# One written order for the loads of SyncE in the SSD and output stages of a decoder-trunk kernel

## The chip, the cores and the metric

The kernel runs on one core of a Trainium2 chip. The metric is device time in microseconds (us), the median of several runs; a profile of one more execution gives the trace. PE is TensorE, ACT is ScalarE, DVE is VectorE, POOL is GpSimd, and SP is SyncE, which here does nothing but issue DMA loads and stores.

## The reference

One layer of a decoder for two request groups: 256 prompt tokens and 8 x 4 sample tokens, so N = 288 columns, model width 2048 = 16 tiles of 128.

```python
mod = silu(c) @ w_ada + b_ada                    # six parts of 2048: sh1, sc1, g1, sh2, sc2, g2
h = rmsnorm(x, norm1) * (1 + sc1) + sh1
u_pool, z, xbc, dt = split(h @ w_in)             # 512, 1536, 2560, 24
pool_out = pool_mixer(u_pool, ...)               # windows 2, 4, 8, 16, a map per group
ssd_out = ssd_mixer(z, xbc, dt, ...)             # conv, softplus(dt), chunked scan, silu(z), rmsnorm
x = x + g1 * (concat([pool_out, ssd_out]) @ w_out)
h2 = rmsnorm(x, norm2) * (1 + sc2) + sh2
x = x + g2 * (silu(dwconv(h2 @ w_gate)) * (h2 @ w_val) @ w_down)
y = rmsnorm(x, norm_f)                           # and new states of pool, conv, SSD and FFN
```

All of it is float32. The weights are some 300 MB, and each is read once.

## The kernel before

**Products.** A float32 product is made of three passes on PE: ACT casts a raw weight half to `whi` (line 329), DVE subtracts it from the raw half to get `wlo` (line 331), and `mm3` (lines 344 to 346) adds `whi*hi`, `whi*lo` and `wlo*hi`. One "half" is 128 x 1024 numbers, 512 KB, loaded by SP at line 310; it serves 8 k-tiles, 24 matmuls.

**Stages.** (1) The first norm and the six blocks of `xbc` over growing k groups, up to some 174 us of the trace. (2) The last block `xbc6`, begun with `mm_dt` (lines 1136 to 1147: the dt weights, 24 columns, are cast by ACT and subtracted by DVE into one tile `whi_dt`, and 32 matmuls read it). Beside `xbc6` and then beside the projections `uz` (z of the groups 2 and 3, `u` of the pooling groups 1 and 0) run the units of `back`: the convolution, the SSD groups 0 to 3 (`ssd_group`, lines 850 to 982), pooling. (3) The output projection, 16 column tiles `mm_out_0` to `mm_out_15`, whose last four k-tiles are those of the pooling groups. (4) The MLP, to the end.

**The ada chunks.** The last four parts of the modulation weights are read in small pieces beside all this. `ada_visits` (line 464) is a generator: it loads four chunks of 512 KB (two k-tiles, two halves each) into the ring `rawa`, later puts a "visit" on PE (`whole`, line 451: 16 matmuls of 512 columns that read these four chunks in the reverse of the order in which they were loaded), and then loads the next four. In the SSD stage the ring `rawa` has just four slots, so the loads of a visit wait until the visit before it has read its chunks. `adap2` and `adap3` are the two parts of this stage, eight visits each; the chunks of `adap3` are `raw_adap_3_0_0` (k-tile 0, half 0) to `raw_adap_3_15_1`. `adap4` has four visits of eight chunks in the output stage.

**What sets the order.** The program is written as generators that are advanced with credits (`pull`, line 1118); a scheduler then reorders each engine's instructions by its own estimate of when they can run, except where `keep_in_program_order` or `in_order` pins them. SP is one queue: a load that waits for its slot holds up every load behind it. Other rings: `raw` (weight halves; four slots and one more in `sx`), `whi` and `wlo` (two slots each). The SSD states `h0` of a group come in three loads (`load_h0`, line 835).

Of the kernel before, what the change touches and what calls it, by code (L numbers as in the profile page):

```python
# [18 lines left out]
P = 128  # L19
# [34 lines left out]
VA = (5.01 / 28, 11.01 / 62, 0.42)  # L54
AK, AO = 2, 4
KQ = 4

RB1, RB2, RB3 = 1.0, 1.0, 1.0
TK = 5
# [65 lines left out]
def _wide(part):  # L125
    return (KT - KQ) * P // 4 if part == 4 else D // 4

# [46 lines left out]
def kernel(ctx: ExitStack, tc, ins, outs):  # L174
# [129 lines left out]

    wp = [None]

    def load(key, ring="raw", eng=nc.sync):
        off, cols = S.items[key]
        t = wp[0].tile([P, RAWC], F32, tag=ring, name="raw_" + "_".join(map(str, key)))
        eng.dma_start(t[:, :cols], wflat[off:off + P * cols].rearrange("(p n) -> p n", p=P))  # L310
        return t

    queue = deque(_need_order())
    ahead = {}
# [41 lines left out]
    def project_units(key, nk, opnd=None, order=None):  # L356

        name = "_".join(map(str, key))
        ps = pm.tile([P, 512], F32, tag="mm", name="mm_" + name)
        for h, (k0, n) in enumerate(_halves(nk)):  # L360
            hi, lo = ready.pop(key + (h,), None) or split(load(key + (h,)), 0, n * P, f"{name}_{h}")
            for i in range(n):
                k = k0 + i
                ko = order[k] if order else k
                bh, bl = (xhi[0][ko], xlo[0][ko]) if opnd is None else opnd(k)
                mm3(ps[:, :N], hi, lo, i, bh, bl, k == 0, k == nk - 1)
                if k % YK == YK - 1 or k == nk - 1:
                    yield ps
# [92 lines left out]
                    tc.keep_in_program_order(i)  # L461
                n += 1

    def ada_visits(parts, step, ps=None, begun=0, apart=False, own=None):

        plan = [(part, k0) for part in parts for k0 in range(begun, KT, step)]
        ahead, end, done = [], None, [0]

        def chunks(v):
            part, k0 = plan[v]  # L470
            for k in range(k0, k0 + step):
                for h in range(2):
                    eng = nc.sync if own is None or done[0] < own else nc.gpsimd
                    ahead.append((k, h, load(("adap", part, k, h), "rawa", eng)))
                    done[0] += 1
                    if apart:
                        yield
            for _ in range(1 if apart else 3):
                yield

        yield from chunks(0)
        for v, (part, k0) in enumerate(plan):
            if end:
                ada_end(*end)
                end = None
            if k0 == 0:
                ps = pa.tile([P, 512], F32, tag="ada", name=f"adap{part}")
            whole(ps, ahead, step, True, begun, _wide(part))
            ahead.clear()
            if k0 + step == KT:  # L490
                end = part, ada_sb(ps, _wide(part), f"p{part}")
            yield
            if v + 1 < len(plan):
                yield from chunks(v + 1)
        ada_end(*end)
        yield

# [152 lines left out]
        nc.vector.tensor_scalar(csr, vec[:, K_TRI:K_TRI + N], 0.0, None, ALU.mult)  # L650

    def late_states():
        nc.sync.dma_start(poolw, ins["pool_w"])
        n = XT * NB * 3
        st = sx[0].tile([P, n + 4 * NB * 15], F32, name="st")
        nc.sync.dma_start(st, ins["st"])
        stc.append(st[:, 0:n].rearrange("p (g m b l) -> p g m b l", g=4, m=5, b=NB))
        nc.gpsimd.tensor_copy(ups.rearrange("p m b l -> p (m b) l")[:, :, 0:15],
                              st[:, n:].rearrange("p (m l) -> p m l", l=15))
# [92 lines left out]
    def xbc_units(bi):  # L752
        (_, gk), _ = BLOCKS[bi]
        end = bi + 1 == len(BLOCKS)
        for ci, (ks, ms) in enumerate(_xbc_chunks(bi)):
            key = ("xbc", bi, ci)
            hi, lo = ready.pop(key, None) or split(load(key) if end else fetch(key), 0, len(ms) * gk * P,
                                                   f"xbc{bi}_{ci}", bi < GB or end)
            begun = []
            if bi + ci == 0:  # L760
                begun = [aux(f"xbc0_{m}") if m % 2 else pm.tile([P, 512], F32, tag="mm", name=f"xbc0_{m}")
# [70 lines left out]
    ssq = kp.tile([P, N], F32, tag="ssx", name="ssq")  # L832
    sbx = kp.tile([P, P + G6], F32, name="sbx")

    def load_h0(g):
        for i, (b0, nb) in enumerate(HB):
            t = mx.tile([P, 3, G6], F32, tag="blk", name=f"h0_{g}_{i}", bufs=4)
            nc.sync.dma_start(t[:, 0:nb, :], ins["h0"][b0:b0 + nb, :, g, :].rearrange("b p n -> p b n"))
            h0t[g, i] = t

    def h0b(g, b):
# [8 lines left out]
    def ssd_group(g):  # L850
# [120 lines left out]
        if g < ZEARLY:  # L971
            nc.scalar.activation(zy[g], zy[g], AF.Silu)
        dec = [decays(0)]
        yield
        dec.append(decays(1))
        outputs(0, *dec[0])
        yield
        dec.append(decays(2))
        outputs(1, *dec[1])
        yield  # L980
        outputs(2, *dec[2])
        yield
# [124 lines left out]
    def take(gn, n):  # L1107
        for _ in range(n):
            next(gn)
            yield  # L1110

    ssd3 = ssd_group(3)
    back = chain(conv0, h0s(0), zip2(ssd_group(0), conv_group(1)), h0s(1),
                 zip2(ssd_group(1), conv_group(2)), h0s(2), zip2(ssd_group(2), conv_group(3)), h0s(3),
                 zip2(take(ssd3, TK), chain(pool_units(UEARLY[0]), pool_units(UEARLY[1]))))
    credit = {}

    def pull(gn, rate):
# [7 lines left out]
    for bi in range(len(BLOCKS)):  # L1126
        last = bi + 1 == len(BLOCKS)
        top_up()
        if last:

            wp[0].drop(w0)
            wp[0].move("rawa", "raw", "rawa")
            w0_ctx.close()
            sx[0] = mx_ctx.enter_context(tc.tile_pool(name="sx", bufs=1, reuse_waits="tile"))
            wp[0].add(sx[0], "raw", "raw", 1)
            raw = load(("dt",))[:, :KT * NH].rearrange("p (k h) -> p k h", h=NH)
            wdt = wp[0].tile([P, RAWC], F32R, tag="whi", name="whi_dt")
            with tc.high_priority():
                nc.gpsimd.memset(wdt.bitcast(F32), 0.0)
                both = wdt[:, :DTW * KT].rearrange("p (k c) -> p k c", c=DTW)  # L1140
                nc.scalar.copy(both[:, :, 0:NH], raw)
                nc.vector.tensor_tensor(both[:, :, 32:32 + NH], raw, both[:, :, 0:NH].bitcast(F32), ALU.subtract)
            ps = pm.tile([P, 512], F32, tag="mm", name="mm_dt")
            for k in range(KT):
                w = wdt[:, DTW * k:DTW * k + P]
                nc.tensor.matmul(ps[:, :N], w, turns(xhi[0][k]), start=k == 0, stop=False)
                nc.tensor.matmul(ps[:, :N], w, turns(xlo[0][k]), start=False, stop=k == KT - 1)
            late_states()
            next(adas)
# [22 lines left out]
    for m in list(range(4 + 3 * ZEARLY, 16)) + ULATE:  # L1172
# [9 lines left out]
        if m < 4:  # L1182
            late[m] = pool_units(m)
            next(late[m])
    drain(adas)
    wp[0].move("rawa", "rawa", "raw")
    adas = ada_visits((4,), AO, apart=True, own=RAWA + RAW2 + RAW3[1])
    for h, (_, n) in enumerate(_halves(KT)):
        ready[("out", 0, h)] = split(load(("out", 0, h)), 0, n * P, f"out_0_{h}")
    drain(back)  # L1190
    npl = kp.tile([P, 4, 135], F32, tag="hmod", name="npl", bufs=2)
    nc.gpsimd.tensor_copy(npl[:, :, 0:15], upp[:, :, NP:15 + NP])
# [14 lines left out]
    def out_units(m):  # L1207
# [1 line left out]
        pz = pm.tile([P, 512], F32, tag="mm", name=f"mm_out_{m}")  # L1209
        pp = aux(f"mm_outp_{m}")  # L1210
        for h, (k0, n) in enumerate(_halves(KT)):
            hi, lo = ready.pop(("out", m, h), None) or split(load(("out", m, h)), 0, n * P, f"out_{m}_{h}")
# [8 lines left out]
    for i in range(KT // YK):  # L1221
# [10 lines left out]
    wp[0].drop(sx[0])  # L1232
# [53 lines left out]
    for m in range(16):  # L1286
        if m in XM:
            sl = slice(4 * XM.index(m), 4 * XM.index(m) + 4)
            nc.sync.dma_start(x[:, sl, :], ins["x"][:, sl, :])
        if m == 1:  # L1290
            wp[0].move("rawa", "raw", "rawa")
            for ring, tag, n in (("rawa", "raw", RAW2), ("whi", "whi", SPLIT2), ("wlo", "wlo", SPLIT2)):
                wp[0].add(w2, ring, tag, n)
            wp[0].add(w3, "raw", "raw", RAW3[0])
            wp[0].add(w3, "rawa", "rawa", RAW3[1])
        if m == 0:
            out_norm(ps0[0], m)
        else:
# [9 lines left out]
            drain(adas)  # L1308


    for k in range(2):
        ready[("upk", k)] = split(load(("upk", k)), 0, 2 * FK * P, f"upk{k}")
    fill = [load(("adaq", q), "rawa") for q in range(KT // 2)]
# [325 lines left out]
```

## Time and profile before

| | us |
|---|---|
| median of 3 runs (range) | 1263.47 (1262.98 to 1264.55) |
| the profiled execution, its own time | 1261.59 |
| its span, first to last instruction | 1259.8 |
| PE busy | 1243.5 (99%) |
| DVE, ACT, POOL busy | 820.7, 581.7, 243.9 |
| mean granted clock of TensorE | 0.998 |

PE is busy nearly all the time, so the time of this kernel is PE's work plus the moments in which PE waits. The rows further down show where these are.

### The profile page before, as it was taken

What the parts mean: (1) busy time and instruction counts of PE and PEld (TensorE: products, weight loads), DVE (VectorE), ACT (ScalarE), POOL (GpSimd) and SP (SyncE); (2) the same over time, 40 slices, a digit from 0 to 9 for tenths busy, and PEclk for the clock granted to TensorE, in tenths of its full rate; (3) what the DMA queues carried; (4) which work ended last, traced back from release to release, by engine and by line L of the source; (5) the groups of instructions that cost most, each with busy time, mean ns of one, the idle gap of its engine ahead of it and who ended that gap; (6) DMA issues with size and microseconds to landing.
All of it is one profiled execution on the core that took longest, in us unless ns stands there. A gap on an engine that the chain in (4) does not pass through costs nothing.

```text
span 1259.8 us, 26442 instructions
## 1 busy us (share of the span) xinstructions
PE 1243.5 (99%) x10647; PEld 1166.6 (93%) x10647; DVE 820.7 (65%) x1379; ACT 581.7 (46%) x914; POOL 243.9 (19%) x468
## 2 busy tenths in 40 slices
PE   9999999999999999999999999999999999999997
PEld 7899988777789899999999999999999999999996
DVE  5785669888776658654675556666665567576553
ACT  5343345688744335433443334444443344444553
POOL 0000003222225413110221001312220012232221
PEclk9999999999999999999999999999999999999999
DMA  9999788888899974788866556665665665666622
GB/s 377 413 415 373 306 290 329 314 306 321 307 372 406 365 263 154 243 321 322 310 210 197 181 194 201 211 208 196 191 195 184 204 206 199 200 216 209 199 75 76
DMA packets 97419, 323.21 MB, mean 257 GB/s; under 512 B 10896, under 2 KB 20048, under 8 KB 97296
## 3 DMA queue, kind: packets, MB, share of 16 engines
q1 hardware_dynamic: 91872, 303.25, 68.8%
q0 software_dynamic: 4704, 17.17, 3.7%
q8 instruction: 83, 1.36, 0.4%
q10 hardware_dynamic: 720, 1.11, 0.2%
q14 instruction: 40, 0.33, 0.1%
HBM read 309.78 MB, written 10.39 MB: 254 GB/s over the span
## 4 chain that ended last, share of the span: by engine, by line
PE 90%; DMA 5%; DVE 2%; ACT 1%; issue 0%; SPq 0%; POOL 0%; DVEq 0%; ACTq 0%; POOLq 0%
PE mm_down L344 7%; PE mm_down L346 7%; PE mm_down L345 7%; PE mm_gate L344 6%; PE mm_val L344 6%; PE mm_gate L345 6%; PE mm_val L345 6%; PE mm_gate L346 6%; PE mm_val L346 6%; PE xbc L344 4%; PE adap L457 4%; PE xbc L345 4%; PE xbc L346 4%; PE adag L419 2%; DMA raw_adap<-wflat 2%; PE mm_out L344 2%
## 5 line engine op out<-in xcount | busy, mean ns | idle before, releaser
L344 PE MATMUL mm_down<-ah,whi_down 128*128 128x288 f32 x688 | 196.8, 286 | 0.0
L345 PE MATMUL mm_down<-al,whi_down 128*128 128x288 f32 x688 | 196.8, 286 | 0.0
L346 PE MATMUL mm_down<-ah,wlo_down 128*128 128x288 f32 x688 | 196.8, 286 | 0.0
L344 PE MATMUL mm_gate<-h2h,whi_gate 128*128 128x288 f32 x640 | 183.5, 287 | 0.0
L344 PE MATMUL mm_val<-h2h,whi_val 128*128 128x288 f32 x640 | 183.1, 286 | 0.0
L346 PE MATMUL mm_gate<-h2h,wlo_gate 128*128 128x288 f32 x640 | 183.0, 286 | 0.0
L345 PE MATMUL mm_val<-h2l,whi_val 128*128 128x288 f32 x640 | 183.0, 286 | 0.0
L346 PE MATMUL mm_val<-h2h,wlo_val 128*128 128x288 f32 x640 | 183.0, 286 | 0.0
L345 PE MATMUL mm_gate<-h2l,whi_gate 128*128 128x288 f32 x640 | 183.0, 286 | 0.0
L331 DVE TENSOR_TENSOR wlo_down<-raw_down,whi_down 128x1024 fp32r<-128x1024 f32 x96 | 108.4, 1129 | 103.2 <-ACT whi_down L329 103.2
L331 DVE TENSOR_TENSOR wlo_gate<-raw_gate,whi_gate 128x1024 fp32r<-128x1024 f32 x80 | 99.8, 1248 | 107.4 <-ACT whi_gate L329 107.4
L329 ACT CAST whi_down<-raw_down 128x1024 fp32r<-128x1024 f32 x96 | 91.9, 957 | 144.0 <-PE mm_down L345 119.9
L329 ACT CAST whi_gate<-raw_gate 128x1024 fp32r<-128x1024 f32 x80 | 83.5, 1045 | 130.3 <-PE mm_gate L345 65.3
L329 ACT CAST whi_val<-raw_val 128x1024 fp32r<-128x1024 f32 x80 | 83.8, 1047 | 115.2 <-issue 91.3
L344 PEld LDWEIGHTS mm_down<-ah,whi_down 128*128 128x128 f32 x688 | 130.0, 189 | 0.0
L345 PEld LDWEIGHTS mm_down<-al,whi_down 128*128 128x128 f32 x688 | 130.0, 189 | 0.0
L346 PEld LDWEIGHTS mm_down<-ah,wlo_down 128*128 128x128 f32 x688 | 130.0, 189 | 0.0
L344 PE MATMUL xbc<-h1h,whi_xbc 128*128 128x288 f32 x444 | 128.9, 292 | 0.8 <-ACT h1h L258 0.5
L345 PE MATMUL xbc<-h1l,whi_xbc 128*128 128x288 f32 x444 | 127.1, 287 | 0.0
L346 PE MATMUL xbc<-h1h,wlo_xbc 128*128 128x288 f32 x444 | 125.2, 287 | 0.3 <-DVE wlo_xbc L331 0.3
L344 PEld LDWEIGHTS mm_gate<-h2h,whi_gate 128*128 128x128 f32 x640 | 120.9, 189 | 3.4 <-issue 3.4
L345 PEld LDWEIGHTS mm_val<-h2l,whi_val 128*128 128x128 f32 x640 | 121.0, 189 | 0.0
(357 smaller groups left out, 3002.9 us busy)
## 6 DMA issues: line engine op xcount, KB each, us to landing
raw_adap<-wflat SPq DMA_DIRECT2D x96, 512.0 KB, 6.1
raw_gate<-wflat SPq DMA_DIRECT2D x80, 512.0 KB, 4.0
raw_val<-wflat SPq DMA_DIRECT2D x80, 512.0 KB, 3.6
raw_ada<-wflat SPq DMA_DIRECT2D x64, 512.0 KB, 9.4
raw_xbc<-wflat SPq DMA_DIRECT2D x50, 512.0 KB, 9.8
raw_down<-wflat SPq DMA_DIRECT2D x48, 512.0 KB, 3.6
raw_out<-wflat SPq DMA_DIRECT2D x32, 512.0 KB, 10.2
raw_down<-wflat SPq DMA_DIRECT2D x32, 384.0 KB, 3.7
```

The costliest lines, as they stand in the source:

```text
L329: yield nc.scalar.copy(hi[:, :n], raw[:, a:a + n])
L331: yield hi, lo, nc.vector.tensor_tensor(lo[:, :n], raw[:, a:a + n], hi[:, :n].bitcast(F32), ALU.subtract)
L344: nc.tensor.matmul(ps, whi[:, w], bh, start=first, stop=False)
L345: nc.tensor.matmul(ps, whi[:, w], bl, start=False, stop=False)
L346: nc.tensor.matmul(ps, wlo[:, w], bh, start=False, stop=last)
L419: i = nc.tensor.matmul(ps[32 * j:32 * j + 32, :nb], sc_c[:, ck, :], raw[:, c:c + nb], start=q0 + n == 0, stop=q0 + AQ[gi] >= nq and n + 1 ...
L457: i = nc.tensor.matmul(ps[32 * j:32 * j + 32, :w], sc_c[:, k, :], raw[:, w * (j % 2):w * (j % 2) + w], start=not begun and k == step - 1, ...
```

## The change

From block `xbc6` to the end of the output projection the loads of SP are pinned in the order in which the program writes them (`tied`). Two helpers keep that order: `plan` is a list of weight halves still to load, `more(n)` loads until n of them are in `coming`, and `came(key)` takes one. A half of `xbc6` or `uz` that is split is followed by `more(4)`, one of `out` by `more(6)`. The chunks of the next visit are loaded right behind the visit that frees their slots, as before, but their loads now keep their place. `load_h0` is called in thirds from within the SSD group before (the first group's states still come from `h0s(0)`). The extra `raw` slot in `sx` is given up a little earlier, and the rings are enlarged in another order in the output stage.

```diff
+LA, OA = 4, 6
     def load(key, ring="raw", eng=nc.sync):
         off, cols = S.items[key]
         t = wp[0].tile([P, RAWC], F32, tag=ring, name="raw_" + "_".join(map(str, key)))
-        eng.dma_start(t[:, :cols], wflat[off:off + P * cols].rearrange("(p n) -> p n", p=P))
+        i = eng.dma_start(t[:, :cols], wflat[off:off + P * cols].rearrange("(p n) -> p n", p=P))
+        if tied[0] and eng is nc.sync:
+            tc.keep_in_program_order(i)
         return t
+    plan, coming = deque(), {}
+    def more(n):
+        while plan and len(coming) < n:
+            key = plan.popleft()
+            coming[key] = load(key)
+    def came(key):
+        while key not in coming:
+            more(len(coming) + 1)
+        return coming.pop(key)
...
-            hi, lo = ready.pop(key + (h,), None) or split(load(key + (h,)), 0, n * P, f"{name}_{h}")
+            half = key + (h,)
+            got = came(half) if half in coming or half in plan else load(half)
+            hi, lo = split(got, 0, n * P, f"{name}_{h}")
+            more(LA)
...
-    def load_h0(g):
-        for i, (b0, nb) in enumerate(HB):
+    def load_h0(g, which=(0, 1, 2)):
+        for i in which if g < 4 else ():
...
         dec = [decays(0)]
+        load_h0(g + 1, (0,))
         yield
         dec.append(decays(1))
         outputs(0, *dec[0])
+        load_h0(g + 1, (1,))
...
             wp[0].add(sx[0], "raw", "raw", 1)
+            tied[0] = True
             raw = load(("dt",))[:, :KT * NH].rearrange("p (k h) -> p k h", h=NH)
...
+            plan.extend(("xbc", bi, ci) for ci in range(len(_xbc_chunks(bi))))
+            plan.extend(("uz", m, h) for m in list(range(4 + 3 * ZEARLY, 16)) + ULATE for h in range(2))
+            plan.extend(("out", 0, h) for h in range(2))
+            more(LA)
             late_states()
...
     drain(adas)
+    wp[0].drop(sx[0])
     wp[0].move("rawa", "rawa", "raw")
...
-        ready[("out", 0, h)] = split(load(("out", 0, h)), 0, n * P, f"out_0_{h}")
+        ready[("out", 0, h)] = split(came(("out", 0, h)), 0, n * P, f"out_0_{h}")
+    plan.extend(("out", m, h) for m in range(1, KT) for h in range(2))
+    more(LA)
```

What it moves on the engines, at three places. First SP at the end of the ada chunks; `raw_out_m_h` is half h of the output weights of column tile m. Before:

```order
L310 DMA raw_out_0_0_4555<-wflat 128x1024
L310 DMA raw_out_0_1_4561<-wflat 128x1024
L310 DMA raw_adap_3_12_0_4380<-wflat 128x1024
L310 DMA raw_adap_3_12_1_4382<-wflat 128x1024
L310 DMA raw_adap_3_13_0_4384<-wflat 128x1024
L310 DMA raw_adap_3_13_1_4386<-wflat 128x1024
L310 DMA raw_out_1_0_4734<-wflat 128x1024
L310 DMA raw_out_1_1_4766<-wflat 128x1024
L310 DMA raw_adap_3_14_0_4470<-wflat 128x1024
```

Now, the same queue and place:

```order
L313 DMA raw_out_0_0_4296<-wflat 128x1024
L313 DMA raw_adap_3_12_0_4388<-wflat 128x1024
L313 DMA raw_adap_3_12_1_4390<-wflat 128x1024
L313 DMA raw_adap_3_13_0_4392<-wflat 128x1024
L313 DMA raw_adap_3_13_1_4394<-wflat 128x1024
L313 DMA raw_out_0_1_4421<-wflat 128x1024
L313 DMA raw_adap_3_14_0_4476<-wflat 128x1024
L313 DMA raw_adap_3_14_1_4478<-wflat 128x1024
L313 DMA raw_adap_3_15_0_4480<-wflat 128x1024
L313 DMA raw_adap_3_15_1_4482<-wflat 128x1024
L313 DMA raw_out_1_0_4567<-wflat 128x1024
```

Half 1 of `mm_out_0` now stands behind the chunks of the last visit but one, and half 0 of `mm_out_1` behind those of the last; before, each stood ahead of them.

Second PE at the same place; a row with `x2` is two matmuls. Before, the last visit but one (chunks 3_13 and 3_12) stands within `mm_uz_0`, the last `uz` tile, and 55 rows of other matmuls follow until the last visit:

```order
L344 MATMUL mm_uz_0_4457<-h1h11_130,whi_uz_0_0_4460 128x288
L457 MATMUL adap3_3684<-raw_adap_3_13_1_4386,sc_c_85 32x512 x2
L457 MATMUL adap3_3684<-raw_adap_3_13_0_4384,sc_c_85 32x512 x2
L457 MATMUL adap3_3684<-raw_adap_3_12_1_4382,sc_c_85 32x512 x2
L457 MATMUL adap3_3684<-raw_adap_3_12_0_4380,sc_c_85 32x512 x2
L345 MATMUL mm_uz_0_4457<-h1l11_146,whi_uz_0_0_4460 128x288
```

Now it stands behind the first half of `mm_out_0`, and these are the rows from it to the last visit and `mm_out_1`, with `...` for nine more matmuls of `mm_out_0` like those around them:

```order
L364 MATMUL mm_out_0_4635<-mixh11_4590,wlo_out_0_0_4561 128x288
L1051 MATMUL pool1_4532<-pout_4120,poolw_153 128x288
L478 MATMUL adap3_3698<-raw_adap_3_13_1_4394,sc_c_85 32x512 x2
...
L478 MATMUL adap3_3698<-raw_adap_3_12_0_4388,sc_c_85 32x512 x2
L362 MATMUL mm_out_0_4635<-mixh12_4591,whi_out_0_1_4563 128x288
...
L364 MATMUL mm_out_0_4635<-mixh15_4594,wlo_out_0_1_4565 128x288
L478 MATMUL adap3_3698<-raw_adap_3_15_1_4482,sc_c_85 32x512 x2
...
L478 MATMUL adap3_3698<-raw_adap_3_14_0_4476,sc_c_85 32x512 x2
L362 MATMUL mm_out_1_4744<-mixh4_4583,whi_out_1_0_4746 128x288
```

Twelve matmuls of `mm_out_0` are all that PE has between the last two visits.

Third DVE ahead of `mm_dt`. `xbc5_24` to `xbc5_27` are the last four tiles of block `xbc5`, which DVE adds to the rows `zy`; `whi_dt` is the subtraction that completes the dt weights. Before:

```order
L331 TENSOR_TENSOR wlo_xbc5_13_2304<-raw_xbc_5_13_2006,whi_xbc5_13_2302 128x1024
L1142 TENSOR_TENSOR whi_dt_2340<-raw_dt_2338,whi_dt_2340 128x16x24
L784 TENSOR_TENSOR zy0_155<-zy0_155,xbc5_24_2274 128x288
L784 TENSOR_TENSOR zy1_156<-zy1_156,xbc5_25_2288 128x288
L331 TENSOR_TENSOR wlo_xbc6_0_2459<-raw_xbc_6_0_2455,whi_xbc6_0_2457 128x1024
L784 TENSOR_TENSOR zy1_156<-zy1_156,xbc5_26_2306 128x288
L784 TENSOR_TENSOR zy1_156<-zy1_156,xbc5_27_2320 128x288
```

Now:

```order
L349 TENSOR_TENSOR wlo_xbc5_13_2304<-raw_xbc_5_13_2006,whi_xbc5_13_2302 128x1024
L812 TENSOR_TENSOR zy0_155<-zy0_155,xbc5_24_2274 128x288
L812 TENSOR_TENSOR zy1_156<-zy1_156,xbc5_25_2288 128x288
L812 TENSOR_TENSOR zy1_156<-zy1_156,xbc5_26_2306 128x288
L812 TENSOR_TENSOR zy1_156<-zy1_156,xbc5_27_2320 128x288
L1175 TENSOR_TENSOR whi_dt_2340<-raw_dt_2338,whi_dt_2340 128x16x24
L349 TENSOR_TENSOR wlo_xbc6_0_2465<-raw_xbc_6_0_2377,whi_xbc6_0_2463 128x1024
```

`whi_dt` moved behind the addition of the last tile of `xbc5`; on PE the 32 matmuls of `mm_dt` still follow at once on that tile.

## Rows read from the trace of the kernel before

**Rows 1.** The page: the span, and each engine's busy time.

```profile
span 1259.8 us, 26442 instructions
PE 1243.5 (99%) x10647; PEld 1166.6 (93%) x10647; DVE 820.7 (65%) x1379; ACT 581.7 (46%) x914; POOL 243.9 (19%) x468
```

**Rows 2.** Stretches: length, busy us (instructions) by engine, clock, DMA share, GB/s.

```profile
200.00:300.00 100.00, 98.62 (x828) 76.54 (x830) 86.18 (x171) 69.49 (x140) 26.07 (x43) 1.00 0.87 318
300.00:340.00 40.00, 38.69 (x348) 29.14 (x341) 30.26 (x58) 30.98 (x71) 7.37 (x10) 1.00 0.84 312
340.00:360.00 20.00, 19.23 (x156) 15.23 (x152) 18.47 (x42) 14.57 (x27) 5.22 (x10) 1.00 0.87 301
620.00:1240.00 620.00, 620.00 (x5051) 620.00 (x5050) 382.00 (x554) 270.71 (x377) 123.44 (x241) 1.00 0.60 193
```

**Rows 3.** Timeline of DVE at `mm_dt`: start, duration, instruction, idle time before.

```profile
171.30 0.55 DVE L1142 TENSOR_TENSOR whi_dt<-raw_dt,whi_dt 128x384 fp32r<-128x384 f32 x1
...
174.89 0.46 DVE L784 TENSOR_TENSOR zy<-zy,xbc 128x288 f32<-128x288 f32 x1 [0.40 <-PE xbc L346]
```

**Rows 4.** Timeline of PE: the last matmul of `xbc5` and the first of `mm_dt`.

```profile
174.57 0.29 PE L346 MATMUL xbc<-h1h,wlo_xbc 128*128 128x288 f32 x1
174.69 0.29 PE L1146 MATMUL mm_dt<-h1h,whi_dt 128*128 128x288 f32 x1
```

**Rows 5.** The chain of waits, 186 to 221 us: start, duration, piece.

```profile
186.26 1.92 PE adap L457 x16
...
188.67 7.49 DMA raw_adap<-wflat
196.20 1.92 PE adap L457 x16
```

**Rows 6.** The chain of waits, 320 to 352 us: visits, and a stretch of ACT.

```profile
323.43 0.54 ACT e L935 x2
323.98 1.28 ACT L936
325.27 0.28 ACT ec L936
...
330.69 1.85 PE adap L457 x16
...
340.93 1.46 PE adap L457 x13
```

**Rows 7.** Timeline of SP from 318 to 346 us: issues of loads.

```profile
331.72 1.75 SPq L310 DMA_DIRECT2D raw_adap<-wflat  x4
333.52 5.27 SPq L310 DMA_DIRECT2D raw_out<-wflat  x2
```

**Rows 8.** Issue to landing: chunks issued at 331.5 to 333.4, weight at 333.5.

```profile
DMA to landing us min/median/max: 3.6/4.9/6.1
...
DMA to landing us min/median/max: 6.9/6.9/6.9
```

**Rows 9.** The tile `raw_out`, 318 to 353 us: min, median, max ns.

```profile
L329 ACT CAST whi_out<-raw_out x3: 1040/1047/1048, 343.1 to 350.5; 128x1024 fp32r<-128x1024 f32 x3
L331 DVE TENSOR_TENSOR wlo_out<-raw_out,whi_out x3: 1210/1214/1217, 344.8 to 351.7; 128x1024 fp32r<-128x1024 f32 x3
```

**Rows 10.** Waits of PE, 180 to 372 us: us in total, times, longest.

```profile
PE pool L1018 <- DVE pout L1012: 1.4, 2, 0.8
```

**Rows 11.** Waits of SP, 180 to 372 us.

```profile
SPq L310 <- PE adap L457: 38.0, 21, 4.4
```

**Rows 12.** Groups by line on ACT, 180 to 380 us.

```profile
L936 ACT ACT_TABLE_LOAD x7 | 9.0, 1283 | 0.1
```

**Rows 13.** Timeline of PE at `mm_out_1`, where half 1 begins.

```profile
361.44 0.29 PE L345 MATMUL mm_out<-mixl,whi_out 128*128 128x288 f32 x1
361.80 0.39 PE L344 MATMUL mm_out<-mixh,whi_out 128*128 128x288 f32 x1
```

**Rows 14.** Issue to landing of `adap4` chunks issued from POOL, 376 to 400 us.

```profile
DMA to landing us min/median/max: 6.2/9.8/14.7
```

More of the change, by code (lines that the diff above doesn't have):

```diff
@@ L305 @@
     wp = [None]
+    tied = [False]
     def load(key, ring="raw", eng=nc.sync):
@@ L462, in whole, with ada_visits, chunk, chunks @@
                 n += 1
[L464 to L478, printed above, removed]
+    def ada_visits(parts, step, ps=None, begun=0, apart=False, own=None, spare=0):
+        visits = [(part, k0) for part in parts for k0 in range(begun, KT, step)]
+        left = deque((part, k0 + k, h) for part, k0 in visits for k in range(step) for h in range(2))
+        ahead, end, done = deque(), None, [0]
+        def chunk():
+            if left:
+                part, k, h = left.popleft()
+                eng = nc.sync if own is None or done[0] < own else nc.gpsimd
+                ahead.append((k, h, load(("adap", part, k, h), "rawa", eng)))
+                done[0] += 1
+        def chunks():
+            for i in range(2 * step):
+                chunk()
+                if apart and i % 2:
+                    yield
+            for _ in range(1 + step if apart else 3):
                 yield
-        yield from chunks(0)
-        for v, (part, k0) in enumerate(plan):
+        for _ in range(spare):
+            chunk()
+        yield from chunks()
+        for v, (part, k0) in enumerate(visits):
             if end:
@@ L487, in ada_visits @@
                 ps = pa.tile([P, 512], F32, tag="ada", name=f"adap{part}")
-            whole(ps, ahead, step, True, begun, _wide(part))
-            ahead.clear()
+            whole(ps, [ahead.popleft() for _ in range(2 * step)], step, True, begun, _wide(part))
             if k0 + step == KT:
@@ L492, in ada_visits @@
             yield
-            if v + 1 < len(plan):
-                yield from chunks(v + 1)
+            if v + 1 < len(visits):
+                yield from chunks()
         ada_end(*end)
@@ L652, in late_states @@
     def late_states():
-        nc.sync.dma_start(poolw, ins["pool_w"])
+        tc.keep_in_program_order(nc.sync.dma_start(poolw, ins["pool_w"]))
         n = XT * NB * 3
         st = sx[0].tile([P, n + 4 * NB * 15], F32, name="st")
-        nc.sync.dma_start(st, ins["st"])
+        tc.keep_in_program_order(nc.sync.dma_start(st, ins["st"]))
         stc.append(st[:, 0:n].rearrange("p (g m b l) -> p g m b l", g=4, m=5, b=NB))
@@ L756, in xbc_units @@
             key = ("xbc", bi, ci)
-            hi, lo = ready.pop(key, None) or split(load(key) if end else fetch(key), 0, len(ms) * gk * P,
+            hi, lo = ready.pop(key, None) or split(came(key) if end else fetch(key), 0, len(ms) * gk * P,
                                                    f"xbc{bi}_{ci}", bi < GB or end)
+            if end:
+                more(LA)
             begun = []
@@ L833 @@
     sbx = kp.tile([P, P + G6], F32, name="sbx")
-    def load_h0(g):
-        for i, (b0, nb) in enumerate(HB):
+    def load_h0(g, which=(0, 1, 2)):
+        for i in which if g < 4 else ():
+            b0, nb = HB[i]
             t = mx.tile([P, 3, G6], F32, tag="blk", name=f"h0_{g}_{i}", bufs=4)
-            nc.sync.dma_start(t[:, 0:nb, :], ins["h0"][b0:b0 + nb, :, g, :].rearrange("b p n -> p b n"))
+            tc.keep_in_program_order(
+                nc.sync.dma_start(t[:, 0:nb, :], ins["h0"][b0:b0 + nb, :, g, :].rearrange("b p n -> p b n")))
             h0t[g, i] = t
@@ L979, in ssd_group @@
         outputs(1, *dec[1])
+        load_h0(g + 1, (2,))
         yield
@@ L1112 @@
     ssd3 = ssd_group(3)
-    back = chain(conv0, h0s(0), zip2(ssd_group(0), conv_group(1)), h0s(1),
-                 zip2(ssd_group(1), conv_group(2)), h0s(2), zip2(ssd_group(2), conv_group(3)), h0s(3),
-                 zip2(take(ssd3, TK), chain(pool_units(UEARLY[0]), pool_units(UEARLY[1]))))
+    back = chain(conv0, h0s(0), zip2(ssd_group(0), conv_group(1)), zip2(ssd_group(1), conv_group(2)),
+                 zip2(ssd_group(2), conv_group(3)), zip2(take(ssd3, TK), chain(pool_units(UEARLY[0]), pool_units(UEARLY[1]))))
     credit = {}
@@ L1188 @@
     for h, (_, n) in enumerate(_halves(KT)):
-        ready[("out", 0, h)] = split(load(("out", 0, h)), 0, n * P, f"out_0_{h}")
+        ready[("out", 0, h)] = split(came(("out", 0, h)), 0, n * P, f"out_0_{h}")
+    plan.extend(("out", m, h) for m in range(1, KT) for h in range(2))
+    more(LA)
     drain(back)
@@ L1211, in out_units @@
         for h, (k0, n) in enumerate(_halves(KT)):
-            hi, lo = ready.pop(("out", m, h), None) or split(load(("out", m, h)), 0, n * P, f"out_{m}_{h}")
+            hi, lo = ready.pop(("out", m, h), None) or split(came(("out", m, h)), 0, n * P, f"out_{m}_{h}")
+            if m:
+                more(OA)
             for i in range(n):
@@ L1231 @@
             _, rstdy = rstd_of(psq, NH * 64, "rstdy")
-    wp[0].drop(sx[0])
     mx_ctx.close()
@@ L1288 @@
             sl = slice(4 * XM.index(m), 4 * XM.index(m) + 4)
-            nc.sync.dma_start(x[:, sl, :], ins["x"][:, sl, :])
+            tc.keep_in_program_order(nc.sync.dma_start(x[:, sl, :], ins["x"][:, sl, :]))
         if m == 1:
-            wp[0].move("rawa", "raw", "rawa")
             for ring, tag, n in (("rawa", "raw", RAW2), ("whi", "whi", SPLIT2), ("wlo", "wlo", SPLIT2)):
                 wp[0].add(w2, ring, tag, n)
+            wp[0].add(w3, "rawa", "rawa", RAW3[1])
+            wp[0].move("rawa", "raw", "rawa")
             wp[0].add(w3, "raw", "raw", RAW3[0])
-            wp[0].add(w3, "rawa", "rawa", RAW3[1])
+            more(OA)
         if m == 0:
@@ L1308 @@
             drain(adas)
+    tied[0] = False
     for k in range(2):
```

## The prediction

> **What bounds the kernel now.** I read the page first, then the table of stretches, then the chain of waits and the timelines of PE, DVE and SP where PE waits. The page says that PE is busy 1243.5 of 1259.8 us [rows 1]. The stretches show where the rest can be: from 620 us on PE never idles, and it runs 5051 matmuls in 620 us, so a matmul of 288 columns costs 0.123 us [rows 2]. The change touches what lies between 174 and some 460 us. There PE is idle 1.38 us between 200 and 300, 1.31 between 300 and 340, and 0.77 between 340 and 360 (length less busy) [rows 2]. Counted from 200 to 360 that is 3.5 us; a matmul behind a wait also takes longer than its pitch, so the whole loss may be some 5 us. That is all that better loads can give back in this stage. On the other side nothing limits what a worse order can cost, since PE, SP and DVE all work in order. So I walked along the new order and asked at each wait which other instruction must end first.
>
> **Part 1, `mm_dt`.** In the trace of before `whi_dt` runs on DVE at 171.30, long ahead of need, and `mm_dt` starts at 174.69, one pitch after the last matmul of `xbc5` at 174.57 [rows 3, 4]. In the new DVE order `whi_dt` stands behind the addition of that very last tile. This addition waits for PE and runs at 174.89 for 0.46 us [rows 3], to 175.35; `whi_dt` then takes its 0.55 us, to 175.90. PE has nothing else there: its next 32 matmuls are `mm_dt`. It starts at some 175.95 and not at 174.69: **+1.3 us**. Nothing takes it back directly: `xbc6` needs `wlo_xbc6_0` only 32 x 0.123 = 3.9 us later, and this takes 1.2 us [rows 9]. Bounds 1.2 and 1.4.
>
> **Part 2, the last two visits.** How fast can one visit follow another? The next four chunks need the slots that a visit frees. In the trace the visit at 330.69 frees them so that SP issues four loads from 331.72 to 333.47 [rows 6, 7]. The last of the four lands 6.1 us after an issue at some 333.05, so at 339.15: 8.5 us after the visit began [rows 7, 8]. The visit reads its chunks in reverse, so its first matmul needs the one that lands last. With other loads in the queue it is slower: the visit at 186.26 was followed by a chunk issued at 188.67 that landed 7.49 us later, and the next visit began at 196.20, 9.9 us after the first [rows 5]. So 8.5 us is the least, 9.9 a poor case. In before the last two visits start at 340.93 and some 10 us later, with 55 rows of matmuls between them, so PE hardly waits for them.
>
> In the new PE order only twelve matmuls of `mm_out_0` stand between them. From the start of the last visit but one PE has 1.9 us of its own matmuls and 12 x 0.123 = 1.5 us, together 3.4; the last visit cannot begin before 8.5. PE idles **+5.1 us** (with 9.9 us it is 6.5; and if half 1 of `mm_out_0`, which lands 1.3 us behind the chunks and then needs a cast, is late, that wait lies inside these 5.1).
>
> Behind the last chunk stands half 0 of `mm_out_1` on SP. The load behind four chunks landed at 333.52 + 6.9 = 340.42, 1.3 us after them [rows 7, 8]. The cast of 1.05 us ends 2.4 us after the visit's start, and PE is through with the visit after 1.9: 0.5 us; `wlo` needs 1.21 us more [rows 9], with two matmuls, four transposes, a pooling matmul and three short ones to fill it. Between 0.5 and 1.5; I take **+0.8**, since the fillers hide about half.
>
> Against it stands what before loses at this place: the 0.77 us of 340 to 360 [rows 2], nearly all of it the pooling matmul that waits 0.8 us for DVE within `mm_out_0` [rows 10]. It now stands behind the first half, 1.2 us and more later, and should find its operand: **-0.8**.
>
> **Part 3, other loads.** Followed by their places in the queue and at 1.3 us each, the weight halves of `xbc6` and `uz` land before their casts, and the loads of `h0` before their use. So the order removes some waits on chunks and on casts in 200 to 340, where PE idles 2.7 us in all [rows 2], but most of those waits are on DVE and ACT in the SSD chain, which the loads don't touch. I take **-1.0**, bounds -3 and +1 (a load behind the head of SP that waits for a visit).
>
> **Part 4, ACT.** One pair more of activation table loads stands on ACT in SSD group 0. A table load takes 1.283 us [rows 12], so ACT has 2.6 us more to do. ACT is busy 69.5 of 100 us between 200 and 300 [rows 2], and the outputs `y` of this group stand later in PE's new order, behind more `uz` matmuls, which hide it: I take 0, and if that cover is not there, +2.6. Beside the row: the ACTIVATE before such a load ends at 323.97, the load runs 323.98 to 325.26, the next starts at 325.27 [rows 6]: nothing lies around it. The Trainium skill ("ScalarE: Activation LUTs", What ACT_TABLE_LOAD costs) has the same 1283 ns for the load, but adds a drain of about 1380 ns at each switch. By that rule the two would cost ACT 5.3 us, an estimate from that page; the trace doesn't show the drain here, so by the row it is 2.6.
>
> **Part 5, output stage.** Where half 1 of `mm_out_1` begins, PE started at 361.80 and not at 361.44 + 0.12 [rows 13], since the cast waits for a `whi` slot; in the new order fewer matmuls stand between the slot's last reader and this place, some three and not eight, so the gap grows by up to 5 x 0.123 = 0.6; but with the halves loaded further ahead other casts come sooner. I take **+0.3**, bounds -0.3 and +0.9. The second visit of `adap4` comes some 14 us after the first instead of 20; its chunks, issued by POOL, take 6.2 to 14.7 us from issue to landing [rows 14], and the third part of them is needed a little after the first. I take 0, at worst +3.
>
> **Sum.** 1.3 + 5.1 + 0.8 - 0.8 - 1.0 + 0.3 = 5.7. The idle 5 us of PE also let DVE and ACT catch up, which run behind at several places in the next 20 us (the gap just named, and a like one at 370); I take 0.7 of that back: **+5.0 us**. Against the profiled execution this is 1261.6 + 5.0 = 1266.6; the median shown is 1.9 us above that execution, so the median would be **1268.5 us**.
>
> **Rivals.**
>
> *The loss in the tail is given back (no change).* What speaks for it: PE idles 3.5 us in the stage now [rows 2], up to 5 with the slower restarts, and most of the waits are small ones which any replanned order could lose. Price: 1.3 + 5.1 + 0.8 + 0.3 less 5 to 7: between +0.5 and +2.5, so 1264 to 1266. Against it: the waits of PE that the trace names are on DVE and ACT results, the pool's 1.4 us being the largest [rows 10]; a new order of SP doesn't shorten these. Chance 0.15.
>
> *The chunks are not bound by the visit (faster).* If chunks 3_14 and 3_15 find free slots before the visit ahead of them is read, for instance in a slot of another ring, part 2 vanishes, its 5.1 and 0.8 alike, and what remains is 1.3 + 0.3 - 0.8 - 1.0 and up to 2 us more of waits that go: -0.2 to -2.5, so 1261 to 1263. For it: slots are moved between the rings in this change. Against it: SP waits 38 us, 21 times, for PE's visits in this stage [rows 11], as it does when the ring holds one visit, and the ring gets no slot. It decides where it takes away over 4 of the 5.1. Chance 0.12.
>
> *More is lost (slower still).* The table loads are not hidden (+2.6), or the second visit of `adap4` is late (+3), or a full queue makes the cycle 9.9 us (+1.4): 1270 to 1273. Chance 0.23.
>
> *The forecast itself:* 0.50, from 1266 to 1270.5.
>
> The measurement tells 0.2% of this kernel, 2.5 us, from no change, so same is 1261 to 1266. The forecast and the last rival are slower (0.73, of which some 0.02 fall to same at the lower edge); the first rival is mostly same, the second half same and half faster, a little more since an order that nobody can see through whole also holds gains that I didn't count. Slower 0.70, same 0.17, faster 0.13. The range leaves out the best cases of the second rival and the worst of the third: 1261.5 to 1273; the likeliest case's own is 1266 to 1270.5.
>
> **What would show it.** In the profile after, `mm_dt` starts some 1.3 us behind the last `xbc5` matmul, with DVE `whi_dt` named as the releaser. The last visit of `adap3` begins 8.5 to 10 us after the one before it, and PE shows one gap of some 5 us (possibly cut in two by half 1 of `mm_out_0`), released by the DMA of `raw_adap`; it is the largest between 180 and 470. The stretch of 20 us around the end of the visits has PE idle near 6 us where it was 0.8. From the last `mm_out` on nothing differs. I am wrong if the two visits lie closer than 7 us, if PE finds other work between them, or if the stretch before them gets over 3 us shorter.

## The result, and the profile after

The changed kernel takes 1276.8 us (median of 6 runs, 1275.96 to 1279.98), the kernel before 1263.5 in the same comparison: a ratio of 1.0105, 95% interval [1.0092, 1.0119]. That is slower, as forecast, but by 13.3 us where 5.0 were forecast, and outside the range. The profiled execution took 1277.76 us, 16.2 us above that of before.

The table of stretches of the changed kernel, columns as in [rows 2]:

```profile
174.00:180.00 6.00, 4.98 (x41) 4.77 (x40) 2.32 (x4) 0.00 (x0) 0.00 (x0) 1.00 0.82 289
180.00:200.00 20.00, 19.47 (x155) 17.43 (x154) 17.76 (x42) 11.42 (x16) 3.32 (x5) 1.00 0.55 208
200.00:300.00 100.00, 95.17 (x796) 73.90 (x794) 81.59 (x166) 66.74 (x130) 28.13 (x46) 1.00 0.84 312
300.00:340.00 40.00, 38.17 (x320) 27.89 (x321) 29.14 (x60) 30.52 (x66) 7.13 (x10) 1.00 0.77 277
340.00:360.00 20.00, 17.53 (x149) 12.97 (x149) 18.61 (x41) 13.92 (x35) 6.97 (x11) 1.00 0.78 293
360.00:380.00 20.00, 15.70 (x103) 11.88 (x103) 6.65 (x10) 7.83 (x10) 0.24 (x1) 0.83 0.81 302
620.00:1240.00 620.00, 620.00 (x5052) 617.22 (x5051) 381.11 (x555) 267.49 (x373) 120.19 (x239) 1.00 0.62 201
```

Two stretches of before that [rows 2] do not have:

```profile
180.00:200.00 20.00, 19.70 (x158) 16.20 (x157) 19.18 (x48) 10.16 (x15) 4.48 (x9) 1.00 0.83 291
...
360.00:380.00 20.00, 19.78 (x167) 17.32 (x166) 11.66 (x25) 6.38 (x9) 7.14 (x14) 1.00 1.03 408
```

PE's idle time (length less busy) is 4.83 us between 200 and 300, where it was 1.38 [rows 2]; 1.83 between 300 and 340 (1.31); 2.47 between 340 and 360 (0.77); and 4.30 between 360 and 380 (0.22). In this last stretch the granted clock is 0.83, not 1.00. Part of the low clock lies in a wait of PE, where it costs nothing (0.93 from 356.26 to 365.46). From 365.46, where PE resumes, to 372 the clock is 0.57 with PE always busy, an estimate of 6.54 x 0.43 = 2.8 us more that PE lost at its lower level:

```profile
365.46:372.00 6.54, 6.54 (x31) 3.16 (x31) 1.96 (x3) 2.91 (x3) 0.00 (x0) 0.57 1.02 411
```

Between 380 and 460 PE idles 0.59 us, where it idled none. From 620 us on nothing differs.

The waits of PE in the changed kernel, 172 to 500 us (in total, times, longest):

```profile
PE adap L478 <- DMA raw_adap<-wflat: 6.5, 2, 4.2
PE cse L960 <- DVE yo L946: 2.3, 2, 1.2
PE pool L1051 <- DVE pout L1045: 2.3, 3, 1.4
PE mm_out L364 <- DVE wlo_out L349: 1.3, 2, 0.7
PE mm_dt L1179 <- DVE whi_dt L1175: 1.0, 1, 1.0
```

The pooling matmul led before, with 1.4 [rows 10]; the waits for chunks and those of `cse` (matmuls of the SSD groups that wait for `yo`, a tile of DVE) were these:

```profile
PE adap L457 <- DMA raw_adap<-wflat: 0.5, 2, 0.4
...
PE cse L930 <- DVE yo L916: 0.4, 1, 0.4
```

So the waits that are named for chunks grew by 6.0 us, and those for results of DVE and ACT by about as much.

DVE at `mm_dt`, after (compare [rows 3]):

```profile
175.28 0.45 DVE L812 TENSOR_TENSOR zy<-zy,xbc 128x288 f32<-128x288 f32 x1 [1.02 <-PE xbc L364]
175.65 0.55 DVE L1175 TENSOR_TENSOR whi_dt<-raw_dt,whi_dt 128x384 fp32r<-128x384 f32 x1
```

`whi_dt` comes right behind the last addition, as read from the order. The end of the ada visits, in the chain of waits, after (compare [rows 6]):

```profile
356.26 1.85 PE adap L478 x16
...
358.75 6.66 DMA raw_adap<-wflat
...
365.46 3.64 PE adap L478 x16
...
369.64 0.24 PE mm_out L363
```

The last visit begins 9.2 us after the one before it. It then takes 3.64 us for the work that took 1.85 before, and the matmuls behind it take 0.24 us for 0.12: PE runs at 1.2 GHz there and not at 2.4. And a place that the prediction did not have, the chain in the SSD stage:

```profile
265.18 1.85 PE adap L478 x16
...
268.40 8.97 DMA raw_adap<-wflat
277.42 1.92 PE adap L478 x16
```

Here the next visit came 12.2 us after the one before, with only 8.9 us of PE work from one start to the next; a chunk took 8.97 us to land. PE stood idle twice in this stretch, 1.1 us for `yo` of DVE and 2.3 us for the chunk.

### The profile page after: what moved, and what is told of

Its sections match the earlier page's. It is cut to its first block, busy times and chain, and to the rows that moved or that the text cites. A ratio compares the mean times of both kernels' runs of the same rounds, so it can differ in the third digit from the quotient of the medians.

```text
span 1276.0 us, 26445 instructions
## 1 busy us (share of the span) xinstructions
PE 1247.6 (98%) x10647; PEld 1167.9 (92%) x10647; DVE 817.8 (64%) x1379; ACT 583.9 (46%) x916; POOL 242.3 (19%) x468
## 4 chain that ended last, share of the span: by engine, by line
PE 87%; DMA 7%; DVE 3%; ACT 1%; issue 1%; SPq 0%; POOL 0%; DVEq 0%; ACTq 0%; POOLq 0%
PE mm_down L362 7%; PE mm_down L364 7%; PE mm_down L363 7%; PE mm_gate L362 6%; PE mm_gate L363 6%; PE mm_val L362 6%; PE mm_val L363 6%; PE mm_gate L364 6%; PE mm_val L364 6%; PE adap L478 4%; DMA raw_ada<-wflat 3%; PE xbc L362 3%; PE xbc L364 3%; PE xbc L363 3%; DMA raw_xbc<-wflat 2%; DMA raw_adap<-wflat 2%
## 6 DMA issues: line engine op xcount, KB each, us to landing
raw_out<-wflat SPq DMA_DIRECT2D x32, 512.0 KB, 10.9
```

## The experiments

**Which half.** First the pins alone, in the SSD stage or in the output stage. `out_tied` sets `tied` only behind the last `uz` tile (h0 and the states are pinned only if `tied`); `ssd_tied` clears it there (and unpins the loads of `x`).

```diff
-            tied[0] = True                  # ahead of load(("dt",))
...
+    tied[0] = True                          # out_tied; ssd_tied: tied[0] = False
     drain(adas)
```

> The loads of the SSD stage are left to the scheduler again (the written plan and the h0 calls in thirds stay, only the pins go); the pins begin where the last uz tile is written. On PE the visits then stand as in the kernel before up to the last but one, and 7.8 us of work stand between the last two (3.4 in the changed kernel). Theory: the loss is made of waits that the pinned order makes in the SSD stage (some 5 us), of the wait for the last visit's chunks (4.4) and of the half clock behind it (some 3); all three go but 0.7 us, so 1264 to 1266 us. Rival: the loss comes from the output stage's loads (plan, more(6), rings in another order), which are still here: 1270 us or more.

Measured: 1261.99 us, ratio to before 0.9987 [0.9977, 0.9997]. With the SSD stage free, the plan, the h0 calls in thirds and the pinned output stage cost nothing; the rival falls.

> The opposite half: loads pinned in the SSD stage as in the changed kernel, free again from the last uz tile on. On PE 6.4 us of work stand between the last two visits, not 3.4. Theory: the waits in the SSD stage stay (5 us and the 1.5 at mm_dt), the wait for the last visit falls to some 2 us and with it, if a short wait leaves the clock alone, the 3 us at half clock: 1270 to 1273 us. Rival (all of the loss is in the output stage): 1264 to 1266.

Measured: 1273.27 us, 1.0077 [1.0061, 1.0093], just above what was expected. PE's longest wait for chunks is 1.6 us and the granted clock stays 1.00. Its chunk waits are 2.3 us in all; the pooling matmuls and `cse` wait 2.3 us each for DVE, as in the changed kernel, so the loss is not made of chunk waits alone. It comes from the pins in the SSD stage; those in the output stage add to it only where the SSD stage is pinned too.

**`mm_dt` alone.** `tied[0] = True` is moved behind the load of the dt weights.

> The load of the dt weights is written ahead of the first pin, so that whi_dt stands ahead of the zy additions on DVE again; 4.9 us of work stand between the last two visits instead of 3.4. Theory: the wait at mm_dt (1.5 us) goes and is a loss of its own, and the tail wait shrinks by 1.5: 1273 to 1275 us. Rival: the PE is later held by the chunks in any case, so that an earlier start is given back: 1276 to 1277.

Measured: 1274.05 us, 2.75 less than the changed kernel, within what was expected, though the intervals of the two ratios (1.0071 to 1.0103, and 1.0092 to 1.0119) overlap. `mm_dt` no longer waits. The tail did not do what was expected of it: PE waited 2.6 us for the chunks of the last visit but one and 3.6 us for those of the last, where the changed kernel waited 4.2 us for the last alone. So `mm_dt` and the tail are not parted by this run. The chain shows both late visits slow now:

```profile
340.65 1.85 PE adap L478 x16
344.05 7.34 DMA raw_adap<-wflat
351.44 3.29 PE adap L478 x16
355.19 7.04 DMA raw_adap<-wflat
362.26 3.64 PE adap L478 x16
```

**The clock.** Matmuls that nobody reads, right behind the last visit but one:

```diff
+            if (part, k0) == (3, 12):
+                ft = aux("fill")
+                for _ in range(24):         # fill40: 40
+                    tc.keep_in_program_order(
+                        nc.tensor.matmul(ft[:, :N], xhi[0][0][:, 0:P], turns(xhi[0][1]), start=True, stop=True))
             yield
```

> Behind the last visit but one stand 24 extra matmuls of 288 columns whose result nobody reads (2.9 us of PE), inside the time in which PE waits for the last chunks anyway; the rest of PE's order is that of the changed kernel but for the pooling matmul pool1. Theory: the long idle stretch lowers the clock, and the last visit and what follows it cost some 3 us more for it; with a shorter idle stretch the granted clock stays 1.00 and the time falls to 1273 to 1274.5 us though PE has more work. Rival: the clock has nothing to do with the idle stretch, and the extra work is hidden or not: 1276.5 to 1280.

Measured: 1275.06 us. PE still waited 3.1 us, and the last visit took 3.61 us. The clock was not kept. The gain of 1.7 us, about half of what was expected, is not clear of noise (1.0080 to 1.0112 against 1.0092 to 1.0119).

> As with 24 extra matmuls, now 40 (4.9 us of PE), so that PE waits less than 2 us for the last chunks. With 24 it still waited 3.1 us and the last visit took 3.6 us for 1.9. Theory: it is the length of PE's idle stretch that sets the clock; the last visit now takes 1.9 to 2.0 us and the time falls to 1272.5 to 1274 us with 2 us more of PE work than before. Rival (the clock falls for another reason): the visit still takes 3.6 us and the time is 1275 or more.

Measured: 1275.74 us. Two stretches of it:

```profile
360.00:365.00 5.00, 2.95 (x24) 1.76 (x26) 0.98 (x2) 0.45 (x1) 0.00 (x0) 1.00 1.02 415
365.00:370.00 5.00, 5.00 (x30) 3.79 (x22) 1.99 (x3) 2.91 (x3) 0.00 (x0) 0.66 1.03 402
```

PE waits only 2.0 us now, the visit begins at full clock and takes 2.46 us, and then the clock falls all the same, with PE busy (5.00 of 5.00, clock 0.66). My theory on the clock, that the length of the wait just ahead sets it, fell; the rival had the time right, and not the visit.

**The loads of h0.** Only `load_h0` is unpinned:

```diff
-            tc.keep_in_program_order(
-                nc.sync.dma_start(t[:, 0:nb, :], ins["h0"][...]...))
+            nc.sync.dma_start(t[:, 0:nb, :], ins["h0"][...]...)
```

> As the changed kernel, with weights, chunks, states and x pinned in the written order; only the twelve loads of h0 are unpinned. The scheduler then issues h0_0_0 to h0_0_2 and h0_1_0 some 35 places earlier on SP, ahead of the chunks of adap2; on PE 7.8 us of work stand between the last two visits. Theory: it is the pinned place of the first h0 loads, right ahead of chunks, that delays the chunks and lets the scheduler bunch the visits; without it the waits of the SSD stage and of the tail go, and mm_dt's 1.5 us stay: 1264 to 1266 us. Rival (the pinned order of weights and chunks itself): 1270 us or more.

Measured: 1263.12 us, 1.0001 [0.9991, 1.0010]: 13.7 us gone by freeing twelve loads out of all that are pinned. Is it the place of the first ones?

```diff
-    back = chain(conv0, h0s(0), zip2(ssd_group(0), ...
+    back = chain(conv0, zip2(ssd_group(0), ...
             late_states()
+            load_h0(0)
             next(adas)
```

> Everything pinned as in the changed kernel, but the three loads of h0_0 are written right behind the states, ahead of the first chunks, not behind the convolution of group 0. 6.2 us of work stand between the last two visits and 8.1 to 8.4 before some others. Theory: the place of h0_0 is most of the loss in the SSD stage (3.5 to 4 of some 7 us with mm_dt), and the tail waits 2 us less: 1268 to 1271 us. Rival (pins of weights and chunks): 1274 us or more.

Measured: 1277.11 us, a clear miss: early is not enough. PE's waits in this kernel show what the loads did there:

```profile
PE adap L478 <- DMA raw_adap<-wflat: 6.9, 4, 4.1
PE xbc L364 <- DVE wlo_xbc L349: 1.7, 1, 1.7
```

They stood in a burst of weights, states and first chunks. The first four chunks took 10.9 to 11.6 us to land, where they took 6.8 to 10.4 in the changed kernel, and `xbc6` waited. The last two visits still bunch, with waits of 1.4 and 4.1 us. The stretch of 156 to 164 us tells the places apart. It is shown for the changed kernel, then before, then `h0_gap`, which is below:

```profile
156.00:164.00 8.00, 8.00 (x101) 6.65 (x103) 4.24 (x7) 2.10 (x2) 0.00 (x0) 1.00 0.31 105
```

```profile
156.00:164.00 8.00, 8.00 (x101) 6.29 (x100) 4.09 (x6) 2.10 (x2) 0.00 (x0) 1.00 0.70 225
```

```profile
156.00:164.00 8.00, 8.00 (x102) 6.29 (x100) 4.09 (x6) 2.10 (x2) 0.00 (x0) 1.00 0.97 353
```

In the changed kernel the DMA engines are busy 31% of these 8 us, since SP waits 7.9 us at the load of `xbc_6_1` for a slot, and no load behind it is issued until then. Pinned loads that have their own free slots can use this stretch only if they stand ahead of that load. Before, one h0 load and the first chunks did. `h0_gap` puts four h0 loads there, with every pin kept (`h0s(0)` is out of `back` here too):

```diff
             tied[0] = True
+            load_h0(0)
+            load_h0(1, (0,))
             raw = load(("dt",))
...
-        load_h0(g + 1, (0,))
+        load_h0(g + 1, (0,) if g else ())
```

> Every load pinned as in the changed kernel; the four loads h0_0_0 to h0_0_2 and h0_1_0 are written ahead of the load of the dt weights (with h0 written behind the states the time was 1277.1, with h0 unpinned 1263.1 and these four loads at this place). Between the load of xbc_6_0 and the next one SP waits some 8 us for a slot, so these transfers meet little else there. Theory: it is the place alone that counts, whoever chose it; in the new order behind that wait the h0 loads share the engines with weights and chunks. Then 1262 to 1265 us. Rival: a pin by itself costs (SP waits that a free order avoids): 1268 or more.

Measured: 1261.59 us, 0.9987 [0.9978, 0.9997]. SP's timeline of this kernel:

```profile
149.11 5.20 SPq L868 DMA_DIRECT2D h<-h  x4
...
156.04 8.99 SPq L313 DMA_DIRECT2D raw_xbc<-wflat  x4
```

The four loads are issued ahead of the wait, and all 13.3 us and 1.9 more are gone, though `mm_dt` still waits its 1.0 us:

```profile
PE mm_dt L1181 <- DVE whi_dt L1177: 1.0, 1, 1.0
PE cse L960 <- DVE yo L946: 0.6, 1, 0.6
PE adap L478 <- DMA raw_adap<-wflat: 0.6, 1, 0.6
```

So a pin costs nothing by itself here, and the place of four loads decides. Two things are not parted by it. `h0_gap` moves one load more than the version before, `h0_1_0`. And PE's order moved with the loads, so it is not shown how much the idle stretch of the DMA engines is worth under one order of PE.

**The tail.** From the version with h0 unpinned and the dt load first (`h0_free_dt`, below), the rate at which visits are pulled is lowered, so that the last two bunch.

```diff
-VA = (5.01 / 28, 11.01 / 62, 0.42)
+VA = (5.01 / 28, 10.51 / 62, 0.42)
```

> From the version with h0 unpinned and the dt load ahead (1260.4 us), the rate at which chunk visits are pulled beside uz is lowered from 11.01 to 10.51 per 62, so that the last two visits stand 2.0 us of PE work apart instead of 7.8; the SSD stage stays well spaced. Theory: the tail by itself costs the 8.5 us cycle less the work between (6.5 us of waiting) and then 2 to 3 us at half clock: 1268 to 1271 us. Rival: the tail's wait is made good by the stages behind it, and the SSD stage made all of the loss: under 1264.

Measured: 1272.81 us, 12.4 us above `h0_free_dt`. The rival falls. The tail is most of it, and not all: of the 9.5 us that PE waited for chunks, 7.5 stand ahead of the last visit, and 1.9 ahead of two earlier visits, which the lower rate moved too; the SSD stage did not stay as it was. Its waits, and two stretches:

```profile
PE adap L478 <- DMA raw_adap<-wflat: 9.5, 3, 7.5
```

```profile
355.00:360.00 5.00, 0.00 (x0) 0.00 (x0) 0.00 (x0) 0.00 (x0) 0.28 (x2) 0.72 0.93 352
360.00:365.00 5.00, 2.80 (x16) 0.60 (x16) 0.38 (x1) 1.04 (x1) 0.00 (x0) 0.50 1.02 410
```

PE does nothing for 5 us and comes back at a granted clock of 0.50, the 1.2 GHz level.

**Versions that gain.** `h0_free_dt` joins the unpinned h0 and the earlier dt load; `h0_free_dt_la3` has `LA = 3` besides; `gap_dt2` pins everything and writes the four h0 loads between the loads of `xbc_6_0` and `xbc_6_1`, with the dt load ahead of the first pin.

> h0 unpinned, and the load of the dt weights written ahead of the first pin, so that whi_dt stands ahead of the zy additions on DVE. Theory: both losses of the written order that were found are gone, the tail has 7.8 us between the last two visits: 1261.5 to 1264 us, the same as the kernel before or just faster. Rival: pinned weights cost something by themselves: 1266 us or more.

Measured: 1260.44 us, 0.9979 [0.9970, 0.9988]: faster than both kernels.

> As the version with h0 unpinned and the dt load ahead, with three halves ahead instead of four; the last two visits then stand 9.0 us apart and the others 9.3 to 14. Theory: with every pair of visits further apart than the 8.5 us cycle there is no chunk wait left, some 0.6 us less: 1259 to 1260.5 us. Rival: three halves ahead leave casts waiting: 1261 to 1264.

Measured: 1262.47 us, 0.9997 [0.9988, 1.0006]. The theory missed; waits of up to 0.7 us for chunks came back at five visits though these stood further apart, which I did not follow up.

```diff
             raw = load(("dt",))[:, :KT * NH].rearrange("p (k h) -> p k h", h=NH)
...
+            tied[0] = True
             plan.extend(...)
+            more(1)
+            load_h0(0)
+            load_h0(1, (0,))
             more(LA)
```

> Every load from xbc_6_0 on pinned, with the written order mended at two places: the load of the dt weights ahead of the first pin, and h0_0_0 to h0_0_2 and h0_1_0 written between the loads of xbc_6_0 and xbc_6_1, where SP waits for a slot. whi_dt then stands ahead of the zy additions on DVE, and the visits as in the version with h0 unpinned (1260.4). Theory: the two places add up and are all of it: 1261.6 less some 1.3 at mm_dt, 1260 to 1261 us, faster than both kernels. Rival: the gains overlap: 1261.5 to 1263.

Measured: 1260.70 us, 0.9982 [0.9973, 0.9991]. Against `h0_gap` 0.9 us are gone by the medians (the intervals overlap), and `mm_dt` no longer stands among PE's waits:

```profile
PE pool L1051 <- DVE pout L1045: 1.0, 1, 1.0
PE y L976 <- ACT ec L966: 0.5, 1, 0.5
PE cse L960 <- DVE yo L946: 0.5, 1, 0.5
PE adap L478 <- DMA raw_adap<-wflat: 0.4, 1, 0.4
```

## Why the prediction was wrong

Point by point, in the profiled executions.

- *`mm_dt`, +1.3.* Right in cause and size: `mm_dt` starts at 176.25, 1.3 us behind the last matmul of `xbc5`, with 1.0 us of named waiting, the releaser DVE `whi_dt`.
- *The last two visits, +5.1 and +0.8 less 0.8.* The 5.1 were right: between the two visits PE waited 0.4, 0.7 and 4.2 us, 5.3 together, and the cycle of chunks was 9.2 us, between the 8.5 and 9.9 read from [rows 5 to 8]. The other two were not. The +0.8 did not come: the matmul of `mm_out_1` that needs `wlo` ran at 371.95 without a wait. The -0.8 was misread: in the trace of before the 0.8 us of [rows 10] stand at 322.27, and the pooling matmul within 340 to 360 waited 0.66. In the changed kernel it waited more, 1.4 us:

```profile
355.51 0.75 PE L1051 MATMUL pool<-pout,poolw 128*128 128x288 f32 x2 [1.36 <-DVE pout L1045]
...
358.48 0.39 PE L362 MATMUL mm_out<-mixh,whi_out 128*128 128x288 f32 x1 [0.36 <-ACT whi_out L347]
...
359.74 0.39 PE L364 MATMUL mm_out<-mixh,wlo_out 128*128 128x288 f32 x1 [0.75 <-DVE wlo_out L349]
...
365.46 3.64 PE L478 MATMUL adap<-raw_adap,sc_c 128*32 128x512 f32 x16 [4.23 <-DMA raw_adap<-wflat]
```

  So the idle time of 340 to 380 rose by 5.8 us (6.77, where before had 0.77 and 0.22), near the 5.1 that was forecast, partly by luck: two misses in part cancel.
- *The clock behind that wait: no term.* This is the first step that failed. I took a wait to cost its own length. Behind it PE also ran at its lower level for the last visit and what followed, some 2.8 us. In before no wait on PE between 180 and 372 us was longer than 0.8 us [rows 10], so no row there showed this. The Trainium skill ("TensorE: Matmul & The Clock Gate", HAM oscillation — how this bites in real kernels) describes a kernel in which the wait for the next operands throttles PE, so that the next piece starts cold. The traces agree where the wait was 2.6 to 7.5 us; I did not weigh it. In `fill40`, with 2.0, the clock fell too, while the visit at 277.42, behind a wait of 2.3 us (6.5 in all, less 4.2), took 1.92 us at full clock.
- *Part 3, other loads, -1.0 with bounds -3 and +1.* This is the step that failed most. I asked of each load whether it lands before its use, found that it does, and stopped. PE's idle time between 180 and 340 rose from 3.0 us (0.30, 1.38 and 1.31) to 7.2, so the term was +4.2. The premise that failed is that the waits on DVE and ACT in the SSD chain are ones "which the loads don't touch". The waits of `cse` for `yo` grew from 0.4 to 2.3 us by the written order, and fell to 0.6 when four loads were moved (`h0_gap`); the waits for chunks grew from 0.5 to 2.3 us here. Two things were missed. The first is what a pin takes away: before, h0 loads went out around SP's wait at 156 to 164; pinned behind it, they are issued later. SP's timeline of the changed kernel shows them between two groups of chunks:

```profile
217.55 1.63 SPq L868 DMA_DIRECT2D h<-h  x3
...
225.30 1.98 SPq L313 DMA_DIRECT2D raw_adap<-wflat  x4
```

  and the four chunks issued at 225.30 take this long (the group issued at 220.86 before took 4.3 to 7.8, the one at 222.49 in `h0_gap` 4.5 to 7.0):

```profile
DMA to landing us min/median/max: 7.8/9.4/10.4
```

  But the visit that reads these chunks, at 239.75, waited for nothing, so no trace shows that this meeting of loads cost PE time.

  The second is what the waits rest on: PE's order was written with those loads where they are, and in it the visits stand later, unevenly, and bunch at the end. From the start of `mm_dt` to the last visit but one PE was busy 163.2 us before, 171.4 in the changed kernel, and 163.0 in `h0_gap`; to the last visit 172.6, 175.3 and 171.3. I had the short distance at the tail and took it for a fact of the tail alone. The visit at 277.42 is the same thing earlier. From the start of the visit ahead of it to its own start PE had this to do, in before and after:

```profile
265.38:278.88 13.50, 13.41 (x121) 10.96 (x121) 9.28 (x17) 12.76 (x28) 0.14 (x1) 1.00 0.96 355
...
265.11:277.42 12.31, 8.85 (x76) 6.21 (x75) 11.89 (x23) 10.54 (x27) 4.38 (x7) 1.00 0.79 272
```

  That is 13.4 us of work and then 8.9, and 13.4 again in `h0_gap`. That the visits are moved by the scheduler's own estimate of the loads is my reading; the runs show only that moving four loads moves both.
- *The gain taken off for DVE and ACT catching up, -0.7; the small terms of part 5; the table loads.* Mostly below what these runs resolve. The 0.59 us of idle time between 380 and 460 stay under the 0.9 that part 5 allowed. No wait on ACT longer than 0.8 us stands among PE's waits.
- *The rivals.* "More is lost" had the right sign but named the table loads, `adap4` and the cycle; none of these was most of it (the cycle was 9.2 us, 0.7 above the least). The chunks are bound by the visits, as part 2 said: `bunch10_51` shows it best.

All the signs that were named for the forecast came true, and none of the signs of being wrong: these looked for a smaller loss, and none for a loss elsewhere.

So the time was, in the profile, 16.2: 1.0 at `mm_dt`, 4.2 in the SSD stage, 5.8 in the tail's waits, 2.8 by the clock, 0.6 between 380 and 460, and 1.8 that I did not follow, slower first matmuls behind waits among them (0.39 us for 0.29).

## What to carry to other kernels

When an in-order queue gets a written order, ask of each moved load not only whether it lands in time but which idle stretch of the transfer engines it used before, and what it now stands behind: a stretch in which the head of the queue waits for a slot is free only for loads written ahead of it. Then read the consumers' new order as a whole, since the scheduler may write it anew around the moved loads: here four loads moved every later visit. Price a long wait on TensorE with the clock behind it, not with its length alone. When the order of consumers shows one bunched place, look for others; here the place of loads 140 us earlier decided it.

## What was not expected of the hardware

After waits of 3.1 to 7.5 us for DMA in the tail, matmuls of 512 columns in the visits took about twice as long (3.61 to 3.66 us for a visit of 1.85 to 1.92), and after the 2.6 us in `dt_first` the visit took 3.29. In `fill40` the clock fell to 0.66 over 5 us in which PE was busy throughout, behind a wait of 2.0 us; in `ssd_tied`, with a longest chunk wait of 1.6 us, it stayed at 1.00. What in the work around the waits decides between these is open; it was not tried further.
